# A decoder layer on one core: small loads on another queue, the residual kept in memory, the last down-projection groups by chunk, parts of x formed later

## The chip, the cores and the metric

The kernel runs on 1 core of one Trainium2 chip. The metric is the device time of one execution in microseconds. The engines are named as in the profile: PE is TensorE (its matmuls; PEld are its weight loads), DVE is VectorE, ACT is ScalarE, POOL is GpSimd, and SP is SyncE, which here does nothing but issue DMAs. ACTq and SPq are the DMA issues of ACT and SP.

## The reference

One layer of a hybrid decoder, for 1024 prompt rows and 8 sample rows (1032 rows in all, model width 1024, feed-forward width 2816), all in float32. The input is normalised first; three token mixers read it through one projection; two residual steps with a norm follow.

```python
xp = layer_norm(x_prompt, ln_in_g, ln_in_b)
xs = layer_norm(x_sample, ln_in_g, ln_in_b)
# in the layer, for each of the two:
proj = x @ w_in + b_in                       # q, k, v, o, gates i and f, u, xq, branch gates
y_m = (norm of sigmoid(o) * mLSTM(q, k, v, i, f)) @ w_m_out
y_p = pool_mix(u)                            # trailing means over 2, 4, 8, 16 rows, @ w_pool
y_x = softmax(xq mk^T) mv @ w_x_out          # mk, mv = mem @ w_mem_kv, or the cache
mix = (g0 * y_m + g1 * y_p + g2 * y_x) @ w_o
x = layer_norm(ALPHA * x + mix, ln1_g, ln1_b)
hup = x @ w_up                               # 2 * 2816 columns
c = causal depthwise convolution of width 3 over hup, + conv_b
a, b = split(c)
f = (gelu(a) * b) @ w_down
x = layer_norm(ALPHA * x + f, ln2_g, ln2_b)
```

The outputs are x for both groups and the new states (mLSTM, pooling, convolution, memory keys and values).

## The kernel before

Activations are kept feature-major: 128 features in the partitions, the 1032 rows in the free dimension, eight such tiles for a width of 1024. Float32 precision comes from splitting each operand in a high and a low part of the matmul's type and adding three products: hi·hi, hi·lo, lo·hi. xhi and xlo are the parts of the current x, whi and wlo (also whl, which holds both halves) those of a weight. The high part is a copy on ACT, the low part a subtraction on DVE (early in the program on POOL too). Rows are handled in three chunks of 384, 384 and 264 (CHUNKS), or, where a layer norm follows, in three passes of 392, 384 and 256 from the last rows to the first (PASSES).

The program is a list of units that PE works off in order (run_units, matmul L258): a unit is one tile of weights times all its chunks. Ahead of time each unit has its weights loaded and split. Between units, generators put in the other work: each step of a generator issues some instructions and yields the microseconds for which it wants to wait, counted against the matmuls issued since. So the yields and the order in which generators were added set the order of instructions on ACT, DVE, POOL and SP; each of these engines works its list off in that order. A DMA issue waits until the DMA issued eight before it in the program has landed, as well as for its data and for its buffer.

The stages, in us from the start of the span: memory keys and values (w_mem_kv) with the input norm beneath them (0 to 80); the w_in projection and the mixers (to 1236); pooling (to 1301); the w_o projection with LN1 beneath it (to 1416); the first three feed-forward tiles as plain units (to 1499); the other nineteen as Strassen products on halves (to 1897); the down-projection with LN2 beneath it (to the end).

What the change touches:

- The small parameter rows, rowsA (L319), eight loads issued by ACT at the start. The rows of x are loaded by SP between the weights of w_mem_kv (raw, L179; x, L311). memT0h, memT0l (L456, L457) are the split transposes of the memory input on ACT and DVE.
- to_features (L381 to L398) transposes normalised rows on PE (L387), applies gain and bias on ACT into tmp (L389) and splits into xhi and xlo. With spill it also writes tmp to memory. It is used for the input norm (no spill) and for LN1 (spill into x1D, eight arrays of 128 x 1032).
- wo_unit (L1378): the evacuation of w_o forms z = ALPHA·(xhi + xlo) + p in two operations on DVE (L1384, L1385). g_rows1 transposes z back to rows (L1398), takes statistics, and normalises on ACT into xn (L1410); few_to_features (L1415 to L1427) does the eight sample rows by themselves: eight small activations xs (L1422) and eight writes into x1D (L1425), all on ACT.
- g_parts (L1660 to L1710): the Strassen products need differences of quarters of x. For four values of k it loads quarters from x1D (wf, L1676), forms three differences on DVE (L1693, L1694, L1700, L1703) and splits them into tx on ACT and DVE (L1684, L1685). last_part (L1715, L1716) splits a fourth one into xhi and xlo once the plain units are done. The evacuation of a plain unit's product is hup (L1527); conv and gelu work on it as cv (L1488 to L1501).
- run_pairs (L1835 on): seven products for each half (L1776), in the order 1, 2, 6, 7, 5, 3, 4, evacuated into t, u, v and hup (L1782 to L1792). The convolution of the pair before goes on beneath them, one step (post) at four of the seven products; its result is written to gD.
- run_down (L1945): w_down in six groups of 4, 4, 4, 4, 2 and 4 tiles of k; a product (L1960) is added into z (z2 in the code, L1970). Groups 0 to 4 run over CHUNKS; group 5 runs pass by pass, so that LN2 of a finished pass (ln2_half, ln2_dev, ln2_out, L1990 to L2045) lies beneath the next. g_stages loads gD and splits it into xhi and xlo (stage, L1885, L1886).

## Time and profile before

| | |
|---|---|
| median of 3 runs | 2180.38 us (2178.87 to 2181.81) |
| the profiled execution | 2181.64 us |
| its span, first to last instruction | 2179.9 us |
| mean granted clock of PE | 0.990 |
| busy: PE, DVE, ACT, POOL | 2123.8, 1296.2, 847.2, 207.7 us |

The page's part of busy time gives each engine's time, its share of the span and its instructions. The list of waits has for each kind of wait what waited, for what, and then us in total, times, and the longest. A row of the timeline is start, length, engine, line and operation, out<-in, shapes and count, and in brackets the idle time before it with what ended it. The table of windows has for each stretch its length, the busy time and the count of PE, PEld, DVE, ACT and POOL, the clock granted to PE (1.00 is full speed), DMA's busy share and GB/s.

### The profile page before, as it was taken

To read this page: it belongs to the slowest core of one execution; us is meant where nothing else is said; L and a number is where in the kernel's file an instruction comes from. 1 tells how busy PE (TensorE), PEld (TensorE's weight loads), DVE (VectorE), ACT (ScalarE), POOL (GpSimd) and SP (SyncE) were. 2 spreads that over 40 slices of the span, in tenths; PEclk is the share of its full clock that TensorE was granted. 3 is DMA by queue.
4 is the path that set the end of the run, shared out by engine and by line. 5 is a ranking of instruction groups with operands and counts; after the bars stand their busy time and mean duration, and the time that the engine had idled before them with its cause. 6 is when DMAs were issued, how large, how long until landed. Compare 5 with 4: busy or idle time off the path is not lost.

```text
span 2179.9 us, 37597 instructions
## 1 busy us (share of the span) xinstructions
PE 2123.8 (97%) x14801; PEld 2081.2 (95%) x14801; DVE 1296.2 (59%) x2922; ACT 847.2 (39%) x1693; POOL 207.7 (10%) x329
## 2 busy tenths in 40 slices
PE   7999999999999999999999999998999999999996
PEld 6999999999999999999999999998999999999996
DVE  5734838383756655425334645748777777755457
ACT  5624343434446533332213333435555555522111
POOL 5301010101000000000003720000000000000004
PEclk9999999999999999999999999999999999999998
DMA  8231232323268575648752322444222222462302
GB/s 244 79 108 54 54 69 62 65 54 79 81 157 278 174 221 173 215 153 313 248 172 85 95 82 78 141 122 136 66 83 79 77 81 79 152 208 69 107 1 78
DMA packets 303837, 265.54 MB, mean 122 GB/s; under 512 B 19405, under 2 KB 275753, under 8 KB 303645
## 3 DMA queue, kind: packets, MB, share of 16 engines
q1 hardware_dynamic: 286763, 244.06, 37.4%
q10 hardware_dynamic: 16898, 19.09, 2.5%
q8 instruction: 116, 1.90, 0.4%
q14 instruction: 60, 0.49, 0.1%
HBM read 197.21 MB, written 66.49 MB: 121 GB/s over the span
## 4 chain that ended last, share of the span: by engine, by line
PE 85%; DVE 6%; DMA 2%; POOL 2%; ACT 2%; issue 2%; SPq 1%; ACTq 0%; POOLq 0%; DVEq 0%
PE pd L258 48%; PE pd L1776 17%; PE pd L1960 10%; PE ps L678 1%; PE ps L679 1%; PE ps L680 1%; DVE wlo L189 1%; DMA ck<-in_cache_mem_k_dram 1%; PE ps L702 1%; DMA Cs<-in_state_C_dram 1%; POOL ps L1286 1%; DMA wf<-x1D 1%; PE ps L387 0%; ACT whi L188 0%; PE ps L883 0%
## 5 line engine op out<-in xcount | busy, mean ns | idle before, releaser
L258 PE MATMUL pd<-xhi,whi 128*128 128x384 f32 (+1 forms) x1872 | 606.8, 324 | 3.3 <-ACT hup L1527 3.3
L258 PE MATMUL pd<-xlo,whi 128*128 128x384 f32 (+1 forms) x1872 | 603.9, 323 | 0.0
L258 PE MATMUL pd<-xhi,wlo 128*128 128x384 f32 (+1 forms) x1872 | 600.9, 321 | 0.0
L258 PEld LDWEIGHTS pd<-xhi,whi 128*128 128x128 f32 x1872 | 353.1, 189 | 12.8 <-issue 8.3
L258 PEld LDWEIGHTS pd<-xlo,whi 128*128 128x128 f32 x1872 | 353.2, 189 | 1.8 <-issue 1.7
L258 PEld LDWEIGHTS pd<-xhi,wlo 128*128 128x128 f32 x1872 | 353.0, 189 | 1.8 <-issue 1.7
L189 DVE TENSOR_TENSOR wlo<-raw,whi 128x512 fp32r<-128x512 f32 (+1 forms) x236 | 166.4, 737 | 275.6 <-ACT whi L188 264.4
L1960 PE MATMUL pd<-xhi,whl 128*128 128x384 f32 (+3 forms) x1056 | 249.1, 322 | 5.0 <-DVE z L1970 5.0
L1776 PE MATMUL pd<-xhi,whl 128*128 128x258 f32 x1216 | 228.0, 285 | 0.5 <-ACT v L1782 0.5
L188 ACT ACTIVATE whi<-raw 128x512 fp32r<-128x512 f32 (+1 forms) x264 | 151.4, 615 | 108.5 <-PE pd L258 80.7
L1776 PEld LDWEIGHTS pd<-xhi,whl 128*128 128x128 f32 x1216 | 192.8, 191 | 0.7 <-ACT v L1782 0.7
L1960 PEld LDWEIGHTS pd<-xhi,whl 128*128 128x128 f32 x1056 | 184.1, 189 | 6.3 <-DVE z L1970 6.2
L1617 ACT ACTIVATE whl<-wf 128x512 fp32r<-128x512 f32 (+1 forms) x181 | 107.7, 617 | 188.3 <-PE pd L1960 145.8
L1776 PE MATMUL pd<-tx,whl 128*128 128x258 f32 x1368 | 172.9, 285 | 3.4 <-DVE hup L1792 2.3
L1776 PE MATMUL pd<-xlo,whl 128*128 128x258 f32 x608 | 173.4, 285 | 2.8 <-DVE xlo L1716 2.7
L1776 PEld LDWEIGHTS pd<-tx,whl 128*128 128x128 f32 x1368 | 168.1, 190 | 4.0 <-DVE hup L1792 2.5
L1960 PE MATMUL pd<-xlo,whl 128*128 128x384 f32 (+3 forms) x528 | 169.7, 321 | 0.2 <-DVE xlo L1886 0.2
L371 POOL TENSOR_TENSOR rs<-rs,half 128x1 f32<-128x1 f32 (+2 forms) x60 | 36.7, 611 | 1218.4 <-DVE rs L370 1187.1
L1618 DVE TENSOR_TENSOR whl<-wf,whl 128x512 fp32r<-128x512 f32 (+1 forms) x181 | 122.0, 675 | 46.5 <-ACT whl L1617 46.1
L1776 PEld LDWEIGHTS pd<-xlo,whl 128*128 128x128 f32 x608 | 116.2, 191 | 3.4 <-DVE xlo L1716 3.4
L1970 DVE TENSOR_TENSOR z<-pd,z 128x384 f32<-128x384 f32 (+3 forms) x120 | 60.9, 513 | 86.5 <-PE pd L1960 86.4
L1814 DVE SCALAR_TENSOR_TENSOR cv<-hup,colB,cv 128x1023 f32<-128x1023 f32 x76 | 97.1, 1278 | 9.7 <-ACT cv L1805 9.7
(558 smaller groups left out, 3747.4 us busy)
## 6 DMA issues: line engine op xcount, KB each, us to landing
raw<-in_w_in_dram SPq DMA_DIRECT2D x72, 512.0 KB
wf<-in_w_up_dram SPq DMA_DIRECT2D x76, 256.0 KB
gD<-cv SPq DMA_DIRECT2D x22, 516.0 KB
wf<-in_w_down_dram SPq DMA_DIRECT2D x40, 256.0 KB
stage<-gD SPq DMA_DIRECT2D x18, 516.0 KB
raw<-in_w_o_dram SPq DMA_DIRECT2D x18, 512.0 KB
mx<-mixD SPq DMA_DIRECT2D x16, 516.0 KB
raw<-in_w_mem_kv_dram SPq DMA_DIRECT2D x16, 512.0 KB
```

The source lines that it names most:

```text
L188: nc.scalar.activation(s.hi[:, ks], s.raw[:, ks], AF.Copy)
L189: (nc.gpsimd if s.pool else nc.vector).tensor_sub(s.lo[:, ks], s.raw[:, ks], raw_f(s.hi[:, ks]))
L258: nc.tensor.matmul(p[:u.m, :n], lhsT=a, rhs=b, start=j == 0, stop=j == len(seq) - 1)
L371: nc.gpsimd.tensor_tensor(out=rs[:n], in0=rs[:n], in1=half[:n], op=OP.pow)
L678: nc.tensor.matmul(out, lhsT=wh, rhs=xh, start=first, stop=False)
L679: nc.tensor.matmul(out, lhsT=wh, rhs=xl, start=False, stop=False)
L1617: nc.scalar.activation(hi, src, AF.Copy)
L1618: nc.vector.tensor_sub(lo, src, raw_f(hi))
L1776: nc.tensor.matmul(p, lhsT=a[:, k], rhs=b, start=onto is None and k + n == 0, stop=k == 3 and n == 2, skip_group_check=onto is not None)
L1814: nc.vector.scalar_tensor_tensor(a, b, w, a, op0=OP.mult, op1=OP.add)
L1960: nc.tensor.matmul(p[:, :n], lhsT=a[:, k], rhs=b, start=k + i == 0, stop=k == nk - 1 and i == 2)
L1970: nc.vector.tensor_add(z, p[:, :n], z)
```

## The change

It has six parts:

1. The eight rowsA loads are issued by SP, behind the load of the first tile of x.
2. The input norm's to_features spills tmp into x0D (eight arrays of 128 x 1032), written by SP; wo_unit reads it back (xr, four buffers, two units ahead), and the evacuation of w_o is one operation on DVE.
3. few_to_features does gain and bias with two operations on DVE, and SP issues its eight writes.
4. g_parts waits 7 instead of 4 after its weights, so its steps come later.
5. In the last Strassen half, the convolution's steps come at two products instead of four.
6. Groups 4 and 5 of the down-projection both run pass by pass, first the eight units of group 4 and then those of group 5 in each pass. The weights of group 4 are kept for all three passes in tiles of the wf pool (whs). The stage loads are issued before, not after, the wait for the group two before. In LN2, the deviation (ln2_dev) of a tile comes ahead of the output of the tile before, and minus_mean (nb) moves into ln2_out.

```diff
@@ load of the parameter rows
-            nc.scalar.dma_start(rowsA[dst:dst + n], as_rows(src))
+            nc.sync.dma_start(rowsA[dst:dst + n], as_rows(src))
@@ to_features
-            tmp = cur[0].tile([128, 392], F32, tag="tmp", bufs=3, name=nm("tmp"))
+            tmp = cur[0].tile([128, 392], F32, tag="tmp", bufs=6 if b0 == LIB else 3, name=nm("tmp"))
...
-                nc.scalar.dma_start(spill[f][:, c0:c0 + n], tmp[:, :n])
+                (nc.sync if b0 == LIB else nc.scalar).dma_start(spill[f][:, c0:c0 + n], tmp[:, :n])
@@ g_ln_in
-            yield from to_features([(xt.pop(i), rows_of(i)) for i in tiles], c0, n, LIG, LIB, 1.0)
+            yield from to_features([(xt.pop(i), rows_of(i)) for i in tiles], c0, n, LIG, LIB, 1.0,
+                                   spill=x0D)
@@ wo_unit
+        def ahead():
+            c0, n = chunk
+            t = X0[c0, f] = cur[0].tile([128, 392], F32, tag="xr", bufs=4, name=nm("xr"))
+            nc.sync.dma_start(t[:, :n], x0D[f][:, c0:c0 + n])
...
-            nc.vector.scalar_tensor_tensor(z, raw_f(xhi[:, f, c0:c0 + n]), ALPHA, p[:, :n], op0=OP.mult, op1=OP.add)
-            nc.vector.scalar_tensor_tensor(z, raw_f(xlo[:, f, c0:c0 + n]), ALPHA, z, op0=OP.mult, op1=OP.add)
+            nc.vector.scalar_tensor_tensor(z, X0.pop((c0, f))[:, :n], ALPHA, p[:, :n], op0=OP.mult, op1=OP.add)
@@ few_to_features
+        nc.vector.tensor_mul(tmp, p[:, :8 * NS].rearrange("p (f b) -> p f b", f=8), by_tile(L1G))
+        nc.vector.tensor_add(tmp, tmp, by_tile(L1B))
         for f in range(8):
-            nc.scalar.activation(tmp[:, f], p[:, f * NS:(f + 1) * NS], AF.Identity,
-                                 bias=colA[:, L1B + f:L1B + f + 1], scale=colA[:, L1G + f:L1G + f + 1])
-        for f in range(8):
-            nc.scalar.dma_start(x1D[f][:, T:], tmp[:, f])
+            nc.sync.dma_start(x1D[f][:, T:], tmp[:, f])
@@ g_parts
         load_weights()
-        yield 4.0
+        yield 7.0
@@ run_pairs
-                if x in (2, 3, 5, 6):
+                if x in ((2, 3, 5, 6) if i < len(halves_) - 1 else (2, 6)):
                     post[:] = [g for g in post if next(g, g) is not g]
@@ g_stages
-            while gi > 1 and gi - 2 not in down_done:
-                yield 1.0
             j0, nk = GROUPS[gi]
             stage[gi] = place["t"].tile([128, 4, TT], F32, tag="t", name=nm("stage"))
...
+            while gi > 1 and gi - 2 not in down_done:
+                yield 1.0
+            if gi == 5:
+                for (c0, n), _ in PASSES:
+                    for k in range(nk):
+                        stage_split(gi, k, c0, c0 + n)
+                        yield 1.0
+                    ready.append(f"stage{gi}_{c0}")
+                return
@@ prepare
+        if o.small:
+            slot = None
+            t = place["wf"].tile([128, HT], F32R, tag="wf", name=nm("whs"))
+            hi, lo = t[:, :n], t[:, n:2 * n]
+            made["hold"] += 1
@@ ln2_out, g_ln2
-        p, mv, rs, nb = LP.pop(t)
+        p, mv, rs = LP.pop(t)
+        nb = minus_mean(mv, rs, m)
...
                 ln2_half(tiles[i], 1)
+                ln2_dev(tiles[i])
+                yield 1.3
             if i:
                 ln2_out(tiles[i - 1], True)
-            if i < len(tiles):
-                ln2_dev(tiles[i])
-            yield 2.4
+                yield 1.3
@@ the list of down units
-    for gi in range(5):
+    for gi in range(4):
...
+    last = [[down_weights(gi, f) for f in range(8)] for gi in (4, 5)]
+    for w in last[0]:
+        w.small = True
     for i, (chunk, tiles) in enumerate(PASSES):
-        for f in range(8):
-            downs.append(Down(5, f, last[f], chunks=(chunk,), last=i == 2))
+        for gi in (4, 5):
+            for f in range(8):
+                downs.append(Down(gi, f, last[gi - 4][f], chunks=(chunk,), last=i == 2))
```

The order of instructions at three places follows, in rows of line, operation, out<-in and size. First ACT at the start of the program before: the eight rowsA loads stand ahead of the copies of the memory input.

```order
L157 ACTIVATE warm<-ident 128x1
L319 DMA rowsA<-in_b_in_dram 32x128
L319 DMA rowsA<-in_b_in_dram 40x128
L319 DMA rowsA<-in_mh_g_dram 8x128
L319 DMA rowsA<-in_pool_scale_dram 8x128
L319 DMA rowsA<-in_ln_in_g_dram 8x128
L319 DMA rowsA<-in_ln_in_b_dram 8x128
L319 DMA rowsA<-in_ln_g_dram 8x128
L319 DMA rowsA<-in_ln_b_dram 8x128
L456 ACTIVATE memT0h_156<-ps_279 128x256
```

And SP at the start of the program after the change (raw is a w_mem_kv load, x a tile of the input).

```order
L179 DMA raw_275<-in_w_mem_kv_dram 128x8x128
L311 DMA x_208_277<-in_x_prompt_dram 128x1024
L319 DMA rowsA<-in_b_in_dram 32x128
L319 DMA rowsA<-in_b_in_dram 40x128
L319 DMA rowsA<-in_mh_g_dram 8x128
L319 DMA rowsA<-in_pool_scale_dram 8x128
L319 DMA rowsA<-in_ln_in_g_dram 8x128
L319 DMA rowsA<-in_ln_in_b_dram 8x128
L319 DMA rowsA<-in_ln_g_dram 8x128
L319 DMA rowsA<-in_ln_b_dram 8x128
L179 DMA raw_333<-in_w_mem_kv_dram 128x8x128
L311 DMA x_224_366<-in_x_prompt_dram 128x1024
```

The eight loads have moved from ACT, where nothing else was being issued, to SP, between the first and the second tile of x.

Second, DVE where the Strassen products begin: the last round of parts (k = 3) and the first xlo of last_part. Before:

```order
L1693 TENSOR_TENSOR wf_16606<-wf_16606,wf_16561 128x516
L1694 TENSOR_TENSOR wf_16561<-wf_16559,wf_16561 128x516
L1618 TENSOR_TENSOR whl_16663<-wf_16392,whl_16663 128x512
L1685 TENSOR_TENSOR tx_16270<-wf_16606,tx_16270 128x516
L1700 SCALAR_TENSOR_TENSOR wf_16559<-wf_16606,wf_16559 128x516
L1608 TENSOR_TENSOR wf_16327<-wf_16327,wf_16408 128x512
L1618 TENSOR_TENSOR whl_16679<-wf_16327,whl_16679 128x512
L1685 TENSOR_TENSOR tx_16269<-wf_16559,tx_16269 128x516
L1703 SCALAR_TENSOR_TENSOR wf_16604<-wf_16559,wf_16604 128x516
L1618 TENSOR_TENSOR whl_16699<-wf_16325,whl_16699 128x512
L1494 SCALAR_TENSOR_TENSOR cv_16656<-hup_16532,colB,cv_16656 128x1023
```

After (L1721, L1722, L1728 and L1731 are the differences, L1713 is tx, L1643 is whl, L1513 a convolution step, L1744 is xlo):

```order
L1721 TENSOR_TENSOR wf_16687<-wf_16687,wf_16646 128x516
L1722 TENSOR_TENSOR wf_16646<-wf_16644,wf_16646 128x516
L1643 TENSOR_TENSOR whl_16743<-wf_16375,whl_16743 128x512
L1513 SCALAR_TENSOR_TENSOR cv_16706<-hup_16573,colB,cv_16706 128x1023
L1713 TENSOR_TENSOR tx_16320<-wf_16687,tx_16320 128x516
L1728 SCALAR_TENSOR_TENSOR wf_16644<-wf_16687,wf_16644 128x516
L1713 TENSOR_TENSOR tx_16319<-wf_16644,tx_16319 128x516
L1731 SCALAR_TENSOR_TENSOR wf_16685<-wf_16644,wf_16685 128x516
L1513 SCALAR_TENSOR_TENSOR cv_16706<-hup_16573,colB,cv_16706 128x1022
L1513 SCALAR_TENSOR_TENSOR cv_16706<-stT,colB,cv_16706 128x8 x2
L1713 TENSOR_TENSOR tx_16321<-wf_16685,tx_16321 128x516
L1744 TENSOR_TENSOR xlo<-wf_16324,xhi 128x516
```

Two weight halves and a weight sum that stood between the steps of this round now stand ahead of it, and the convolution step that stood behind the second difference now stands ahead of the first tx.

Third, DVE at the end of the Strassen products: cv is the convolution of the pair before, xlo here the split of the first stage for the down-projection, and the hup from v the evacuation that frees the products' bank. Before:

```order
L1814 SCALAR_TENSOR_TENSOR cv_21473<-hup_21069,colB,cv_21473 128x1022
L1814 SCALAR_TENSOR_TENSOR cv_21473<-stT,colB,cv_21473 128x8
L1903 TENSOR_TENSOR xlo<-wf_21379,xhi 128x516
L1828 TENSOR_TENSOR cv_21473<-cv_21395,cv_21473 128x1032
L1903 TENSOR_TENSOR xlo<-wf_21433,xhi 128x516
L1792 SCALAR_TENSOR_TENSOR hup_21317<-pd_21520,v_21549 128x258
L1903 TENSOR_TENSOR xlo<-wf_21435,xhi 128x516
```

After:

```order
L1931 TENSOR_TENSOR xlo<-wf_21429,xhi 128x516
L1842 SCALAR_TENSOR_TENSOR cv_21523<-hup_21119,colB,cv_21523 128x1023
L1842 SCALAR_TENSOR_TENSOR cv_21523<-stT,colB,cv_21523 128x8
L1931 TENSOR_TENSOR xlo<-wf_21483,xhi 128x516
L1820 SCALAR_TENSOR_TENSOR hup_21367<-pd_21567,v_21594 128x258
L1842 SCALAR_TENSOR_TENSOR cv_21523<-hup_21119,colB,cv_21523 128x1022
L1842 SCALAR_TENSOR_TENSOR cv_21523<-stT,colB,cv_21523 128x8
L1931 TENSOR_TENSOR xlo<-wf_21485,xhi 128x516
```

The product of the two convolution halves (L1828) has moved behind this hup, out of these rows.

More of the change, by code (lines that the diff above doesn't have):

```diff
@@ L415, in g_rows_in @@
             yield 2.8
+    x0D = [DR(f"x0D{f}", [128, TT]) for f in range(8)]
     def g_ln_in():
@@ L1383, in evac @@
             z = Z[c0, f] = ZT[c0, f // per][:, f % per * n:(f % per + 1) * n]
-            nc.vector.scalar_tensor_tensor(z, raw_f(xhi[:, f, c0:c0 + n]), ALPHA, p[:, :n], op0=OP.mult, op1=OP.add)
-            nc.vector.scalar_tensor_tensor(z, raw_f(xlo[:, f, c0:c0 + n]), ALPHA, z, op0=OP.mult, op1=OP.add)
-        return Unit(split, col, 8, mov_mix, evac, chunks=(chunk,))
+            nc.vector.scalar_tensor_tensor(z, X0.pop((c0, f))[:, :n], ALPHA, p[:, :n], op0=OP.mult, op1=OP.add)
+        return Unit(split, col, 8, mov_mix, evac, chunks=(chunk,), ahead=ahead)
     XN = {}
@@ L1446, in tile_hybrid_step @@
             if i == 0 and j == 0:
-                on(units[-1], "before", lambda: next_phase("phase2"))
+                first_wo = units[-1]
         on(units[-1], "after", lambda t=tiles, i=i, c0=chunk[0]: (side.add(0, f"rows1{i}", g_rows1(c0, t)),
@@ L1450, in tile_hybrid_step, with open_wo @@
     on(units[-1], "after", lambda: side.add(0, "sconv", g_state_conv()))
+    def open_wo():
+        next_phase("phase2")
+        for u in two:
+            u()
+    two = [u.ahead for u in units[units.index(first_wo):][:2]]
+    for u in units[units.index(first_wo):][:2]:
+        u.ahead = None
+    on(first_wo, "before", open_wo)
     CA, TL = {}, {}
@@ L1561, in __init__ @@
             self.src, self.w, self.f, self.steps = src, {}, {}, steps
-            self.sums = 0
+            self.sums, self.small = 0, False
     def wf_tile(n=512):
@@ L1598, in prepare @@
     def prepare():
-        if made["obj"] == len(wq) or not slots:
+        if made["obj"] == len(wq) or not (slots or wq[made["obj"]].small):
             return False
@@ L1611, in prepare @@
             return False
-        slot = slots.pop(0)
-        t = (wp if slot == "w" else place["ex"]).tile([128, 1024], F32R, tag="w", name=nm("whl"))
         src = o.f[key]
         n = src.shape[1]
-        hi, lo = t[:, :n], t[:, 512:512 + n]
+        if o.small:
[3 more added lines that the diff above has]
+            made["hold"] += 1
+        else:
+            slot = slots.pop(0)
+            t = (wp if slot == "w" else place["ex"]).tile([128, 1024], F32R, tag="w", name=nm("whl"))
+            hi, lo = t[:, :n], t[:, 512:512 + n]
         nc.scalar.activation(hi, src, AF.Copy)
@@ L1635, in release @@
     def release(o, key):
-        slots.append(o.w[key][2])
+        if o.small:
+            made["hold"] -= 1
+        else:
+            slots.append(o.w[key][2])
     def x_part(m, k, s):
@@ L1953, in run_down @@
             if u.f == 0 and (u.gi or c0):
-                wait_for(f"stage{u.gi}")
+                wait_for(f"stage{u.gi}" if u.gi < 5 else f"stage5_{c0}")
             p = pp.tile([128, 512], F32, tag="d", bufs=3, name=nm("pd"))
@@ L2011, in ln2_dev @@
         mv, rs = mean_dev(st, 2, m)
-        LP[t] = p, mv, rs, minus_mean(mv, rs, m)
+        LP[t] = p, mv, rs
     def ln2_out(t, slow):
         m = rows_of(t)
-        p, mv, rs, nb = LP.pop(t)
+        p, mv, rs = LP.pop(t)
+        nb = minus_mean(mv, rs, m)
         y = R("y")
@@ L2034, in g_ln2 @@
                 ln2_half(tiles[i], 1)
+                ln2_dev(tiles[i])
+                yield 1.3
             if i:
                 ln2_out(tiles[i - 1], True)
-            if i < len(tiles):
-                ln2_dev(tiles[i])
-            yield 2.4
-    last = [down_weights(5, f) for f in range(8)]
+                yield 1.3
+    last = [[down_weights(gi, f) for f in range(8)] for gi in (4, 5)]
+    for w in last[0]:
+        w.small = True
     for i, (chunk, tiles) in enumerate(PASSES):
-        for f in range(8):
-            downs.append(Down(5, f, last[f], chunks=(chunk,), last=i == 2))
+        for gi in (4, 5):
+            for f in range(8):
+                downs.append(Down(gi, f, last[gi - 4][f], chunks=(chunk,), last=i == 2))
         if i == 0:
```

2 lines of the change are left out of this document (added).

## The prediction

> **What bounds the kernel now.** I read first the busy times, then the list of what TensorE waits for, then the granted clock of the stretches behind the long waits.
>
> ```profile
> PE 2123.8 (97%) x14801; PEld 2081.2 (95%) x14801; DVE 1296.2 (59%) x2922; ACT 847.2 (39%) x1693; POOL 207.7 (10%) x329
> ```
>
> TensorE is busy 97% of 2179.9 us and the change leaves its matmuls as they are. So what can be won is idle time of PE, time at half clock, and the tail. The waits, as us in total, times, longest:
>
> ```profile
> PE ps L454 <- DVE memT0l L457: 8.2, 1, 8.2
> PE ps L387 <- ACT xn L1410: 5.8, 2, 3.2
> PE pd L1960 <- DVE z L1970: 5.0, 3, 2.9
> PE pd L258 <- ACT hup L1527: 3.3, 1, 3.3
> PE pd L1776 <- DVE xlo L1716: 2.7, 2, 1.5
> PE ps L2005 <- DVE z L1970: 2.4, 2, 1.9
> PE pd L1776 <- DVE hup L1792: 2.3, 1, 2.3
> ...
> PE ps L1398 <- DVE z L1385: 1.0, 2, 0.6
> ```
>
> Every edit aims at one of these rows. Behind each long wait there are stretches of 3.4 us, or two of them, at half clock (columns: length, busy time and count of PE, PEld, DVE, ACT and POOL, clock, DMA share, GB/s):
>
> ```profile
> 1359.50:1366.30 6.80, 5.95 (x20) 5.85 (x21) 3.59 (x8) 4.87 (x8) 0.00 (x0) 0.50 0.45 121
> 1475.50:1478.90 3.40, 3.40 (x13) 3.40 (x12) 3.37 (x6) 0.84 (x2) 0.00 (x0) 0.50 0.65 205
> 1509.70:1516.50 6.80, 6.04 (x28) 6.04 (x29) 5.79 (x10) 1.81 (x4) 0.00 (x0) 0.50 0.45 132
> 1895.40:1898.80 3.40, 3.18 (x14) 3.18 (x15) 1.57 (x4) 3.21 (x6) 0.00 (x0) 0.50 0.96 303
> 2141.20:2144.50 3.30, 2.87 (x9) 2.88 (x10) 3.12 (x5) 0.78 (x1) 2.37 (x2) 0.50 0.30 117
> ```
>
> A matmul takes twice its time there, so such a stretch costs half of PE's busy time in it: 3.0, 1.7, 3.0, 1.6 and 1.4 us.
>
> **A. Small loads to SP.**
>
> ```profile
> 14.34 0.28 ACTq L319 DMA_DIRECT2D rowsA<-in_ln_b_dram  x1
> 14.67 1.21 ACT L456 ACTIVATE memT0h<-ps 128x256 fp32r<-128x256 f32 x4 [12.37 <-DMA rowsA<-in_ln_in_g_dram]
> ...
> 9.40 0.43 SPq L179 DMA_DIRECT2D raw<-in_w_mem_kv_dram  x1
> ...
> 39.94 0.33 PE L387 MATMUL ps<-ident,x 128*128 128x128 f32 x1 [1.86 <-DVE x L375]
> ```
>
> ScalarE issues its last rowsA load at 14.34 and only then begins memT0h, for which PE waited 8.2 us from 7.38. Without its DMAs it can begin there: 14.67 - 7.38 = 7.3 us earlier at most. But SP now stands in those waits: in the program each issue waits on the semaphore that the DMA eight before it raises when it has landed, so the fifth w_mem_kv load, behind the eight, goes out at about 14.6 instead of 9.40. Every load behind it falls back too, by less and less as the queue fills again, and so does x, whose third tile PE waits for at 39.94. That tile cannot come the full 7.3 us earlier; between 0 and 7.3 I take 5, since the loads lose part of the delay again. PE, 7.3 us ahead, waits for it longer than now and gets a half-clock stretch (1.7 by the 3.4-us rows above); the x loads that then queue behind writes of x0, which wait for ScalarE's tmp, may cost 0 to 1.5, I take 0.8. 5 - 1.7 - 0.8 = **2.5**, bounds 0 and 7.3.
>
> **B. Residual from memory, and C. few_to_features off ScalarE.**
>
> ```profile
> 1355.37 0.60 ACT L1422 ACTIVATE xs<-ps,colA 128x8 f32<-128x8 f32 x2
> ...
> 1357.09 2.38 ACTq L1425 DMA_DIRECT2D x1D<-xs  x5
> 1359.52 1.44 ACT L1410 ACTIVATE xn<-ps,nb,rs 128x512 f32<-128x512 f32 x2 [2.05 <-DVE z L1385]
> ...
> 1360.35 0.48 PE L387 MATMUL ps<-ident,xn 128*128 128x128 f32 x1 [3.17 <-ACT xn L1410]
> ...
> 1320.00:1340.00 20.00, 20.00 (x117) 19.71 (x116) 9.53 (x18) 2.25 (x4) 0.00 (x0) 1.00 0.25 72
> ```
>
> From 1355.37 to 1359.47 ScalarE does eight small activations and eight issues while xn stands behind them; PE idles 3.17 us and then runs 6.8 us at half clock (3.0). With two DVE operations and SP's issues instead, xn can start some 2.7 us earlier (its row names 2.05 us of idle time that falls away as well), which about closes the gap: 6.2. The z wait of 1.0 goes with the second STT. On the other side: eight writes of 0.48 us each (2.38 / 5) now stand on SP before the next w_o load, 3.8 us; PE is not waiting for w_o loads here, so between 0 and 3.8, near 0: I take 0.5. The first w_o loads also stand behind two reads of x0D. The other xn gap of the 5.8 (2.6 us) stays, and the free phase of the clock's stretches can give it a drop it did not have (1.7, about two in three: 1.1). The 4.2 MB written and 4.2 MB read (8 x 128 x 1032 x 4 bytes) lie in stretches like the last row, where DMA is 25% busy: nothing. Against the 7.2: 0.5 + 1.1 and 0.6 for the loop's rest. **5.0**, bounds 2 and 7.2.
>
> **D. Parts of x later.**
>
> ```profile
> 1461.15 2.89 SPq L1573 DMA_DIRECT2D wf<-in_w_up_dram  x4
> ...
> 1467.55 0.70 DVE L1693 TENSOR_TENSOR wf<-wf,wf 128x516 f32<-128x516 f32 x1 [8.65 <-DMA wf<-x1D]
> ...
> 1473.73 0.47 ACT L1527 ACTIVATE hup<-pd 128x384 f32<-128x384 f32 x1
> ...
> 1502.70 0.38 ACT L1782 ACTIVATE t<-pd 128x258 f32<-128x258 f32 x1
> ...
> 1505.77 0.69 DVE L1716 TENSOR_TENSOR xlo<-wf,xhi 128x516 fp32r<-128x516 f32 x1
> ...
> 1467.50:1505.70 38.20, 33.75 (x220) 33.19 (x220) 34.98 (x54) 22.29 (x43) 0.00 (x0) 0.96 0.49 146
> ```
>
> The evacuation hup at 1473.73 stands behind two tx copies that wait for DVE; PE's 3.34 us gap and the 1.7 of clock come from that. Now the copies stand behind hup, so hup comes about 1.5 to 2.7 us earlier. But this does not set the end of the stage. DVE does: it is busy 34.98 of the 38.20 us from 1467.55 to the first xlo, for which PE waits again (1.5 and 1.2 us), and ScalarE's t, behind the last tx, makes the first tx matmul wait. The same work must be done before those, and DVE now starts on weight halves, whose four loads stand on SP behind the x1D loads (1461.15): some 2 us after 1467.55 (an estimate: 4 x 256 KB at the 303 GB/s of the 1895.40 row take 3.5 us, part of which is over by then). Two wlo that stood behind its first step, 0.6 us each by their 512 columns (xlo above, 516, takes 0.69), go ahead of it. The last round of tx (last k) ends up in one row behind everything, each step going DVE to ScalarE to DVE; the x1D loads for it are issued only after the round before. I count 2 us of late start, 1.2 saved, and 0 to 4 us more idle time in these handoffs, of which I take 2.2: xlo 3 us later on the same scale. PE, earlier by the gap that closed, idles it all away before the first tx matmul; that long idle time has its half clock inside the wait, which gives back half of the 3.0. **-1.5**; at best +5 (3.34 and 1.7 all kept), at worst -5.
>
> **E. Last Strassen half.**
>
> ```profile
> 1893.40 1.22 DVE L1828 TENSOR_TENSOR cv<-cv,cv 128x1032 f32<-128x1032 f32 x1
> ...
> 1895.15 0.41 DVE L1792 SCALAR_TENSOR_TENSOR hup<-pd,v 128x258 f32<-128x258 f32 x1
> ...
> 1895.62 0.58 PE L1776 MATMUL pd<-tx,whl 128*128 128x258 f32 x1 [2.32 <-DVE hup L1792]
> ```
>
> PE's matmuls feeding that hup end at 1893.3. In the new order the multiply cv (1893.40) no longer stands ahead of it; a convolution step and two xlo still do. hup comes some 1.1 us earlier, the gap falls to 1.2. With half of the idle time gone the half clock (1.6) should not follow: **2.6**, bounds 0 and 3.9. The clock stood at 0.50 right behind a gap of 2.32 us. The Trainium skill ("TensorE: Matmul & The Clock Gate", "Why this matters for your kernels") asks for no idle gaps above about 3 us; by it the 2.32 us would have cost no clock, and E would be 1.1 and the time 2169.8. The trace disagrees in this place. That page's Part 1 calls the window free-running, 3413 ns long, and with that the 3.4 us stretches agree.
>
> **F. Last two groups by chunk.**
>
> ```profile
> 2135.09 0.55 POOL L371 TENSOR_TENSOR rs<-rs,half 128x1 f32<-128x1 f32 x1 [0.94 <-DVE rs L370]
> ...
> 2140.36 0.55 POOL L371 TENSOR_TENSOR rs<-rs,half 128x1 f32<-128x1 f32 x1 [0.94 <-DVE rs L370]
> ...
> 2135.75 0.55 DVE L1970 TENSOR_TENSOR z<-pd,z 128x384 f32<-128x384 f32 x1
> ...
> 2166.38 1.10 PE L2005 MATMUL ps<-ident,z 128*128 128x128 f32 x6 [0.50 <-DVE z L1970]
> ```
>
> A tile of LN2 takes 5.27 us (2135.09 to 2140.36); four take 21.1, the middle pass has 8 x 12 matmuls at about 0.175 us (the last row of B has 117 in 20.00 us), 16.8. So z, behind nb and y on DVE, comes late, up to the 2.91 us in the waits. With group 4 in the pass there are 8 x 6 matmuls more (8.4 us) and eight z of 0.55 (4.4): 25.5 of DVE under 25.2 of matmuls, and the transposes beside them. The waits (5.0 + 2.4) should halve, not vanish, since tiles still come early in a pass; a drop of the clock is as likely as now. The tail behind 2167.48, 12.4 us, has the same operations. **3.5**, bounds 0 and 9 (7.4 and 1.4).
>
> **Sum.** 2.5 + 5.0 - 1.5 + 2.6 + 3.5 = 12.1. Against the profiled execution, 2181.64: 2169.5; the runs' median, 2180.38, lies 1.26 below that execution, so **2168.3**.
>
> **Rivals.**
> - *DVE keeps pace in D.* The handoffs fit into its 3.2 us of idle time and the closed gap is kept: +5 for -1.5, 2161.8. Against it: 35 of 38 us busy.
> - *Front and end give it back.* SP's late loads eat all of A, the z waits move instead of halving: 2174.3. For it: the queue of A, and DVE as full under the passes as before.
> - *It does not do what it says:* D at -5, A and F nothing, B and C 2.5, E 1.1: -1.4 and 2181.8.
> - *Slower: weights run dry in the first pass.* Sixteen weights must be there within 25.8 us of matmuls (8 x 18 at 0.179, the 0.175 by 392/384). If they come one by one, at up to 2.7 us each (four w_up loads issued at 1461.15, the last in use at 1471.97 at the latest), 43 us are needed and PE loses 17: 2185.6. It decides once more than 16 us come through. Against it: the whole of group 3 ahead, 8 units of 12 matmuls on each chunk, some 45 us, in which they can be loaded.
>
> **Numbers.** Forecast 0.52, DVE keeps pace 0.13, given back 0.17, nothing 0.12, slower 0.06. A measurement here tells apart about 0.2%, 4.4 us: faster 0.82 (the first three), same 0.12, slower 0.06. The range runs from below the second case into the fourth, 2158 to 2180, and leaves out the slower case, much of the fourth and the outer bounds of D and F.
>
> **What would show it.** Right: the L454 wait is gone and an x wait on L387 near 30 us has grown; no 3.17 us gap beside xs; the hup wait, some 8 us earlier than now, below 2 us, but PE waiting 5 us or more for t just before the first tx matmul; the hup L1792 wait near 1.2 us with full clock behind it; z waits of 3 to 4 us in all. Wrong: a t wait under 2 us (D gains), a wait for whl or whs at L1960 (the slower case), or raw loads named in waits between 1300 and 1416 (B and C smaller).

## The result, and the profile after

| | before | after |
|---|---|---|
| median of 4 runs | 2180.72 us (2178.87 to 2181.81) | 2162.50 us (2161.90 to 2166.63) |
| ratio after / before | | 0.992, 95% interval 0.9905 to 0.9936 |
| profiled execution | 2181.64 us | 2166.63 us |
| its span | 2179.9 us | 2164.5 us |

The change is 18.2 us faster in the medians; 12.1 had been forecast (2168.3 us), and the time lies in the range. The profiled execution is the longest of the four after the change, so the traces show only 15.4 us of span; where the rest lies is told with the first experiment.

The page's busy times after the change, then the list of what PE waits for (us in total, times, longest):

```profile
PE 2120.8 (98%) x14801; PEld 2080.7 (96%) x14801; DVE 1282.9 (59%) x2908; ACT 847.3 (39%) x1693; POOL 211.3 (10%) x329
```

```profile
PE pd L1804 <- ACT t L1810: 8.2, 1, 8.2
PE ps L387 <- DVE x L375: 6.4, 3, 4.5
PE pd L1995 <- DVE z L2005: 3.0, 2, 2.1
PE ps L387 <- ACT xn L1419: 2.4, 1, 2.4
...
PE pd L258 <- ACT hup L1546: 1.8, 1, 1.8
...
PE pd L1804 <- DVE hup L1820: 0.8, 1, 0.8
...
PE ps L2040 <- DVE z L2005: 0.2, 1, 0.2
```

The 8.2 us for memT0l is gone, and an x wait of 4.5 has come. Of two xn waits one is left. The last hup (L1820, before L1792) cost 2.3 and costs 0.8. The z waits fell from 7.4 to 3.2. Against this stands one new row at the top: PE waits 8.2 us for t, just ahead of the first tx matmul.

PE runs 14801 matmuls in every version, and up to the last two groups in the same order. So the start of the same matmul in two traces can be subtracted, and a stage's gain is how that difference grows over the stage. This table is worked out in that way from the profiled executions, in us against before (minus is gained): A from 0 to 60 us, the mixers to 1300, B and C (w_o and LN1) to 1460, D to 1516, E to 2010 (E's own place, 1885 to 1899, with nothing else happening behind it), F to the last matmul, and the tail behind it (12.4 us before). The runs below the first row are the experiments.

```
                        A mixers    B+C      D      E      F   tail   span
after                -3.8    0.1   -4.7    2.4   -3.3   -4.6   -1.5  -15.4
e0_after             -4.2    3.3   -9.1    3.1   -3.2   -6.2   -1.5  -17.8
e1_parts_early       -4.2    2.3   -9.0   -1.7   -3.2   -4.7   -1.4  -21.9
e2_rows_on_act        2.1    1.0   -7.6    3.5   -3.2   -6.2   -1.5  -11.9
e3_post_four         -3.9   -2.4   -4.8    2.7   -0.2   -4.7   -1.4  -14.7
e4_down_before       -2.6    2.0   -6.1    2.4   -3.2    1.3    0.0   -6.2
e5_few_on_act        -3.8    3.2   -1.0    3.1   -3.3   -4.7   -1.5   -8.0
e6_residual_split    -3.7   -2.3   -6.4    2.4   -3.3   -6.2   -1.2  -20.7
e7_ln2_before        -3.5   -1.6   -9.0    2.5   -3.3   -2.1    0.0  -17.0
e8_chunk_before      -2.8    2.2   -9.2    2.6   -3.3   -7.7   -1.5  -19.7
e9_rows_later        -3.4    2.0   -8.9    0.1   -3.3   -6.2   -1.4  -21.1
e10_t_first          -3.8    3.1   -6.4    2.7   -3.2   -4.7   -1.5  -13.8
e11_all              -4.8    1.0   -5.7   -1.0   -3.2   -4.7   -1.4  -19.8
```

The mixers' column, where the change does nothing, shows how far one profiled execution can be trusted: it runs from -2.4 to 3.3.

### The profile page after: what moved, and what is told of

The parts are those of the page before. It is cut to its first block, busy times and chain, and to the rows that moved or that the text cites. A ratio compares the mean times of both kernels' runs of the same rounds, so it can differ in the third digit from the quotient of the medians.

```text
span 2164.5 us, 37648 instructions
## 1 busy us (share of the span) xinstructions
PE 2120.8 (98%) x14801; PEld 2080.7 (96%) x14801; DVE 1282.9 (59%) x2908; ACT 847.3 (39%) x1693; POOL 211.3 (10%) x329
## 4 chain that ended last, share of the span: by engine, by line
PE 85%; DVE 5%; DMA 4%; ACT 2%; SPq 1%; issue 1%; POOL 1%; ACTq 0%; DVEq 0%; POOLq 0%
PE pd L258 48%; PE pd L1804 18%; PE pd L1995 11%; PE ps L681 2%; PE ps L682 1%; PE ps L683 1%; DMA g2r<-gD 1%; SPq L179 1%; PE ps L705 1%; DMA x<-in_x_prompt_dram 1%; DMA Cs<-in_state_C_dram 1%; POOL ps L1289 1%; PE ps L387 1%; DVE cv L1513 1%; DVE wlo L189 1%
## 5 line engine op out<-in xcount | busy, mean ns | idle before, releaser
L1995 PE MATMUL pd<-xhi,whl 128*128 128x384 f32 (+3 forms) x960 | 225.5, 321 | 3.0 <-DVE z L2005 3.0
L1804 PEld LDWEIGHTS pd<-xhi,whl 128*128 128x128 f32 x1216 | 190.6, 189 | 1.0 <-ACT v L1810 0.7
L1995 PEld LDWEIGHTS pd<-xhi,whl 128*128 128x128 f32 x960 | 167.5, 189 | 3.6 <-DVE z L2005 3.5
L1642 ACT ACTIVATE whl<-wf 128x512 fp32r<-128x512 f32 x173 | 104.4, 626 | 158.6 <-PE pd L1995 117.8
L1995 PE MATMUL pd<-xlo,whl 128*128 128x384 f32 (+3 forms) x480 | 154.3, 321 | 0.0
L1643 DVE TENSOR_TENSOR whl<-wf,whl 128x512 fp32r<-128x512 f32 x173 | 118.8, 687 | 47.9 <-ACT whl L1642 47.5
```

Source lines behind the costliest of these rows:

```text
L1642: nc.scalar.activation(hi, src, AF.Copy)
L1643: nc.vector.tensor_sub(lo, src, raw_f(hi))
L1804: nc.tensor.matmul(p, lhsT=a[:, k], rhs=b, start=onto is None and k + n == 0, stop=k == 3 and n == 2, skip_group_check=onto is not None)
L1995: nc.tensor.matmul(p[:, :n], lhsT=a[:, k], rhs=b, start=k + i == 0, stop=k == nk - 1 and i == 2)
```

## The experiments

Each kernel is the changed one with one part undone or moved. Kernels that did not run side by side are compared through their ratio to runs of before on the same chip.

**The changed kernel again**, with no edit.

> The changed kernel once more, as the measure for the runs beside it. Both theories: 2162 to 2164 us, 0.992 of the kernel before. If the 2166.6 of the profiled execution was only the phase of the clock's windows, single times near 2166 turn up here too.

Measured: 2164.66 us against 2182.74, ratio 0.9926 (0.991 to 0.9943). Single executions ran from 2162.37 to 2172.70 us, so times near 2166 do turn up. Its trace is 2.4 us shorter than the first one, with B and C at 9.1 instead of 4.7 and F at 6.2 instead of 4.6 (and 3.2 lost in the mixers). The windows of the two tell why (columns as before: the clock is the third number from the end). First execution, then this one (a drop is a stretch in which this clock is lower):

```profile
1392.50:1395.90 3.40, 3.40 (x20) 3.40 (x19) 2.99 (x6) 1.94 (x4) 0.00 (x0) 0.58 0.22 81
1426.50:1433.30 6.80, 6.80 (x37) 6.39 (x36) 3.19 (x11) 1.68 (x3) 0.00 (x0) 0.55 0.24 80
2144.40:2147.80 3.40, 3.40 (x20) 3.40 (x20) 0.77 (x2) 0.00 (x0) 0.23 (x1) 0.56 0.20 77
```

```profile
1392.50:1395.90 3.40, 1.51 (x13) 1.51 (x14) 1.65 (x5) 2.15 (x4) 0.00 (x0) 1.00 0.64 193
1426.50:1433.30 6.80, 6.80 (x57) 6.25 (x56) 3.77 (x13) 2.26 (x4) 0.00 (x0) 1.00 0.34 114
2144.40:2147.80 3.40, 3.40 (x31) 3.40 (x31) 2.01 (x4) 0.00 (x0) 0.00 (x0) 1.00 0.20 77
```

The same program got about half clock in these places in one execution and full clock in the other. The first two windows cost 0.42 x 3.4 + 0.45 x 6.8 = 4.5 us and the third 0.44 x 3.4 = 1.5: the differences of B and C (4.4) and of F (1.6). So a stage's gain has to be read with the drops that fell into it.

**D undone: parts of x early.**

```diff
-        yield 7.0
+        yield 4.0
```

> The changed kernel with the parts of x formed as early as before (wait 4 instead of 7). Theory 'DVE sets the start of the Strassen products': faster than the changed kernel by 2 to 4.5 us (2158 to 2160.5), the wait for t falls from 8.2 to 1 to 2 us, the hup wait grows from 1.8 to 3.3 us. Rival 'the closed hup gap is kept': slower by 3 to 5 us (2165.5 to 2167.5).

Measured: 2161.00 us, ratio 0.9903 (0.9888 to 0.9918), 3.7 below the changed kernel in the same comparison; the intervals still touch. D goes from +2.4 or +3.1 to -1.7. The waits there, after the edit:

```profile
PE pd L258 <- ACT hup L1546: 3.6, 1, 3.6
...
PE pd L1804 <- DVE xlo L1744: 2.7, 2, 1.5
...
PE pd L1804 <- ACT t L1810: 1.3, 1, 1.3
```

The early hup wait is back at 3.6 (3.3 before the change), but only 1.3 of the 8.2 us for t stays. So part 4 trades 1.8 us of one wait (3.6 to 1.8) for 6.9 of another, less 2.7 for xlo. That is a loss of 2.4 in waits alone. The clock adds to it. The two windows behind the long wait in the changed kernel, and the one behind the 1.3 us after the edit:

```profile
1499.50:1503.00 3.50, 2.31 (x10) 2.31 (x11) 3.46 (x7) 3.27 (x7) 0.00 (x0) 0.50 0.14 41
1503.00:1506.30 3.30, 3.30 (x19) 3.30 (x19) 3.30 (x7) 2.87 (x5) 0.00 (x0) 0.60 0.34 95
```

```profile
1492.00:1495.50 3.50, 2.85 (x23) 2.86 (x24) 3.46 (x6) 3.50 (x10) 0.00 (x0) 1.00 0.88 291
```

With PE busy for 2.31 us at 0.50 and 3.30 at 0.60, 0.50 x 2.31 + 0.40 x 3.30 = 2.5 us go; with the early parts none. 2.4 + 2.5 = 4.9, beside 4.1 to 4.8 by the table. The two later runs with early parts (e9_rows_later, e11_all) have D at 0.1 and -1.0: each had a drop of 3.4 us behind its xlo waits. So part 4 loses 2.3 to 5.2 us between any two of these traces.

**The last third part behind t**, with the late start kept.

```diff
             split(6, k, x11)
...
-            split(4, k, x21)
+            if k < 3:
+                split(4, k, x21)
+            else:
+                later.append(lambda: split(4, 3, x21))
...
     def last_part():
         k = last_part.k
+        if k == 1:
+            later.pop()()
```

> The changed kernel with its late start of the parts of x, but the last round's third part is rounded after ScalarE has copied t, not before. Theory (t waits its turn on ScalarE behind the last handed-off part, and that part alone comes about 2 us behind the one that TensorE needs): the wait for t falls from 8.2 to about 6.5 us, the kernel is 1.5 to 2 us faster than the changed one. Rival (t only stands where the sixth product's own part would hold TensorE anyway): the wait keeps its length under another name, the time within 0.5 us of the changed kernel.

Measured: 2167.58 us, ratio 0.9926 (0.9906 to 0.9946), the same as the changed kernel. Its list of waits has:

```profile
PE pd L1810 <- ACT t L1816: 6.5, 1, 6.5
...
PE pd L1810 <- DVE xlo L1750: 0.9, 1, 0.9
```

The first half of the theory held: the wait fell by 1.7 us. The second did not: D is +2.7, as in the other runs with the late start (2.4 to 3.5). PE starts earlier and is stopped again at xlo, which stands behind the same work: its waits for t, xlo and hup in the stage are 9.8 us in all, where the changed kernel has 10.0. ScalarE's rows in the changed kernel show what the stage waits for:

```profile
1493.99 0.63 ACT L1712 ACTIVATE tx<-wf 128x516 fp32r<-128x516 f32 x1 [1.32 <-DVE wf L1721]
1497.73 0.63 ACT L1712 ACTIVATE tx<-wf 128x516 fp32r<-128x516 f32 x1 [3.10 <-DVE wf L1728]
...
1499.73 0.63 ACT L1712 ACTIVATE tx<-wf 128x516 fp32r<-128x516 f32 x1 [1.09 <-DVE wf L1731]
1500.27 0.37 ACT L1810 ACTIVATE t<-pd 128x258 f32<-128x258 f32 x1
```

Three tx copies of the last round, each behind a difference from DVE, together with ScalarE's waits for them, fill the time from 1492.67 to 1500.27, with ScalarE idle for 5.5 us of it. DVE's rows, first where it comes to the weights, then the first difference and the first xlo, and the window between these two:

```profile
1461.26 0.69 DVE L1607 TENSOR_TENSOR wf<-wf,wf 128x512 f32<-128x512 f32 x1 [4.20 <-DMA wf<-in_w_up_dram]
...
1462.47 0.69 DVE L1721 TENSOR_TENSOR wf<-wf,wf 128x516 f32<-128x516 f32 x1
...
1501.81 0.69 DVE L1744 TENSOR_TENSOR xlo<-wf,xhi 128x516 fp32r<-128x516 f32 x1
```

```profile
1462.40:1501.80 39.40, 29.26 (x179) 28.56 (x178) 33.18 (x51) 20.06 (x39) 0.00 (x0) 0.88 0.40 122
```

DVE is busy 33.18 of 39.40 us, so 6.2 idle, where between the same two operations it was busy 34.98 of 38.20 before, 3.2 idle. PE's matmuls come 8.4 us earlier here than before the change when this stage begins, so the first difference, at 1467.55 before, is 3.3 us late against them, and the first xlo, at 1505.77 before, 4.4 us late. Neither engine is full: the handoffs from one to the other are in a row and begin too late.

**A undone: rows on ScalarE.**

```diff
-            nc.sync.dma_start(rowsA[dst:dst + n], as_rows(src))
+            nc.scalar.dma_start(rowsA[dst:dst + n], as_rows(src))
```

> The changed kernel with the eight rowsA loads issued by ACT again. Theory 'A is worth the difference between memT0h starting early and x coming late': slower by 2.5 to 4 us (2165 to 2166.5), L457 waits again 8 us, the x wait near 30 us falls from 4.5 to about 2. Rival 'the queue of SP gives all of it back': within 1 us of the changed kernel.

Measured: 2170.07 us, ratio 0.9947 (0.9935 to 0.9959), 5.4 above the changed kernel and more than the 2.5 to 4 expected. The memT0l wait is back with 8.0 us, and the x waits are 4.2 in all (longest 1.9). A is +2.1 instead of about -3.8. So the move of the rows alone is worth 5.4 (the medians) to 5.9 us. Against before, the front even loses 2.1 here; the new writes of x0D are the only other change in it, though with the rows on SP nothing is gained by leaving them out (B undone, below).

**Rows still on SP, but behind the third x tile** (with the parts of x early).

```diff
                 load_x(0)
-                load_rows()
                 mem_transposes()
...
                 load_x(2)
+                load_rows()
```

> The row loads on SyncE are issued behind the third x tile instead of the first (and the parts of x are formed as early as before the change). Theory (SyncE stands in the row loads while x tiles 1 and 2 wait, and that is why the x wait near 30 us stays at 4.5 to 6.2 us): that wait falls to under 3 us and the kernel gains 1.5 to 3 us on the variant with the parts formed early alone (2161.0): 2158 to 2159.5. Rival (x comes late because the memory system is full, not because of who is in front): the wait stays at 4.5 to 6 us, the time at 2160 to 2162.

Measured: 2161.58 us, ratio 0.9901 (0.9884 to 0.9917), as the variant with early parts alone. The theory fell: the x wait is 5.1 us, within the 4.5 to 6.9 of the runs that leave this part as it is. The timeline tells where it comes from. SP and DVE in the changed kernel:

```profile
14.66 1.05 SPq L311 DMA_DIRECT2D x<-in_x_prompt_dram  x2
15.75 9.32 SPq L179 DMA_DIRECT2D raw<-in_w_mem_kv_dram  x5
25.19 1.66 SPq L311 DMA_DIRECT2D x<-in_x_prompt_dram  x1
```

```profile
25.05 1.79 DVE L375 TENSOR_SCALAR x<-x,mv,rs 128x1024 f32<-128x1024 f32 x1 [0.17 <-POOL rs L371]
31.77 1.29 DVE L363 BATCH_NORM_STATS2 st<-x 128x6 f32<-128x512 f32 x2 [4.93 <-DMA x<-in_x_prompt_dram]
...
33.41 0.80 DVE L375 TENSOR_SCALAR x<-x,mv,rs 128x1024 f32<-128x1024 f32 x1
```

And with the rows behind the third tile:

```profile
9.81 1.89 SPq L311 DMA_DIRECT2D x<-in_x_prompt_dram  x2
...
18.59 6.40 SPq L179 DMA_DIRECT2D raw<-in_w_mem_kv_dram  x5
25.11 1.53 SPq L311 DMA_DIRECT2D x<-in_x_prompt_dram  x1
```

```profile
31.11 1.29 DVE L363 BATCH_NORM_STATS2 st<-x 128x6 f32<-128x512 f32 x2 [5.49 <-DMA x<-in_x_prompt_dram]
...
32.75 0.80 DVE L375 TENSOR_SCALAR x<-x,mv,rs 128x1024 f32<-128x1024 f32 x1
```

The loads of the second and third tile went out 4.9 us earlier and nothing came of it. In g_rows_in the statistics of a tile (L363) stand ahead of the normalisation of the one before (L375). So DVE waits for the fourth tile before it normalises the third, for which PE waits. The fourth is issued at 25.1 us in both, behind five raw loads in which SP stands (9.32 us, or 6.40 when it comes to them later). That the fourth tile sets the wait is read from these rows; a kernel with the two operations in the other order was not run.

**C undone: the eight sample rows on ScalarE.**

```diff
-        nc.vector.tensor_mul(tmp, ...)
-        nc.vector.tensor_add(tmp, tmp, by_tile(L1B))
         for f in range(8):
-            nc.sync.dma_start(x1D[f][:, T:], tmp[:, f])
+            nc.scalar.activation(tmp[:, f], p[:, f * NS:(f + 1) * NS], AF.Identity, ...)
+        for f in range(8):
+            nc.scalar.dma_start(x1D[f][:, T:], tmp[:, f])
```

> The changed kernel with few_to_features' eight activations and eight writes on ACT again. Theory 'they stood ahead of xn': slower by 4 to 6.5 us (2168.5 to 2171 where the changed kernel has 2164.7), a wait of about 3 us for xn at L1419 comes back beside them, with half clock behind it. Rival 'that gap was the loop of ACT and DVE in LN1, not the small work': slower by at most 2 us.

Measured: 2170.63 us, ratio 0.996 (0.9945 to 0.9975), by the ratios 7.4 us above the changed kernel, somewhat more than expected. The gap of before is back, in the same place:

```profile
1356.90 2.32 ACTq L1434 DMA_DIRECT2D x1D<-xs  x5
1359.27 1.44 ACT L1419 ACTIVATE xn<-ps,nb,rs 128x512 f32<-128x512 f32 x2 [2.05 <-DMA x1D<-xs]
```

```profile
1360.10 0.33 PE L387 MATMUL ps<-ident,xn 128*128 128x128 f32 x1 [3.15 <-ACT xn L1419]
```

B and C together gain 1.0 in this trace, where the others have 4.7 to 9.2. By the traces C is worth 3.7 to 8.2 us, by how many drops of the clock fall into the stage.

**B undone: the residual from xhi and xlo.**

```diff
-            nc.vector.scalar_tensor_tensor(z, X0.pop((c0, f))[:, :n], ALPHA, p[:, :n], ...)
+            nc.vector.scalar_tensor_tensor(z, raw_f(xhi[:, f, c0:c0 + n]), ALPHA, p[:, :n], ...)
+            nc.vector.scalar_tensor_tensor(z, raw_f(xlo[:, f, c0:c0 + n]), ALPHA, z, ...)
...
-                                   spill=x0D)
```

> The changed kernel without x0D: the residual from xhi and xlo in two operations again, nothing written or read. Theory 'the second STT costs its one wait of 0.6 us': slower by 0.3 to 1.5 us, the x wait near 30 us unchanged. Rival 'the 8.4 MB and the place of the writes on SP cost something': faster by 1 to 3 us, with smaller x waits between 30 and 65 us.

Measured: 2163.54 us, ratio 0.9924 (0.9909 to 0.9939), the same as the changed kernel. A z wait of 0.9 us in all is back in LN1; in the front the two small x waits (0.6 and 1.3) are gone. The long one is 6.0, within the 4.5 to 6.9 of the runs that keep x0D. B moves some two microseconds about and is worth nothing that can be measured.

**E undone: the convolution at four products in the last half** (profiled, without an interval).

```diff
-                if x in ((2, 3, 5, 6) if i < len(halves_) - 1 else (2, 6)):
+                if x in (2, 3, 5, 6):
```

> The changed kernel with the convolution's steps at four products in the last Strassen half again. Theory: the wait for hup at L1820 goes from 0.8 back to 2.3 us and 3.4 us of half clock stand behind it; the stretch is 3 us longer. Rival 'the clock's drop was chance': 2.3 us of wait and full clock behind it, 1.5 us longer.

Measured: 2167.0 us, span 2165.1. E falls from 3.3 to 0.2, by 3.1. The wait for hup is 2.3 us as before, and the two windows behind it are, in the changed kernel and then here:

```profile
1885.80:1889.20 3.40, 2.56 (x21) 2.36 (x21) 2.94 (x7) 3.08 (x7) 0.00 (x0) 1.00 1.05 321
1889.20:1892.60 3.40, 3.40 (x22) 3.40 (x22) 3.40 (x7) 3.40 (x7) 0.00 (x0) 1.00 1.21 300
```

```profile
1885.80:1889.20 3.40, 2.37 (x14) 2.37 (x15) 2.57 (x7) 3.40 (x7) 0.00 (x0) 0.84 0.78 240
1889.20:1892.60 3.40, 3.40 (x15) 3.40 (x15) 2.83 (x6) 1.62 (x5) 0.00 (x0) 0.66 1.07 317
```

1.5 us of the gain is the wait (2.3 to 0.8); the other 1.7 = 0.16 x 3.4 + 0.34 x 3.4 is the clock, which does not drop behind the shorter gap. Both traces with the old order had this drop; the last section shows why a gap of 2.3 us can also go without one.

**F undone, whole and in halves.** Part 6 of the change has two edits: which units run in which pass, and the order inside LN2. First both undone:

```diff
-    for gi in range(4):
+    for gi in range(5):
...
-        for gi in (4, 5):
-            for f in range(8):
-                downs.append(Down(gi, f, last[gi - 4][f], chunks=(chunk,), last=i == 2))
+        for f in range(8):
+            downs.append(Down(5, f, last[f], chunks=(chunk,), last=i == 2))
...
-                ln2_dev(tiles[i])
-                yield 1.3
             if i:
                 ln2_out(tiles[i - 1], True)
-                yield 1.3
+            if i < len(tiles):
+                ln2_dev(tiles[i])
+            yield 2.4
```

> The changed kernel with the down-projection and LN2 of before (group 4 over all chunks, old order in LN2). Theory 'the longer passes cover LN2': slower by 4 to 7 us (2166.5 to 2169.5), z waits 7 us again, half clock near the middle pass. Rival 'it was only the phase of the clock': slower by at most 2 us and z waits as in the changed kernel, 3 us.

Measured: 2175.44 us, ratio 0.9968 (0.9957 to 0.9979), 10.8 above the changed kernel: more than expected. F with its tail goes from -6.1 or -7.7 (the two traces of the changed kernel) to +1.3.

Then only the order inside LN2 undone (the last lines of the diff above, and minus_mean back in ln2_dev):

> The changed kernel with the old order inside LN2 (deviation after the output of the tile before, nb with the deviation), groups 4 and 5 by chunk as in the change. Theory 'the longer passes do it': slower by 0 to 2.5 us, z waits 3 to 5 us. Rival 'the order in LN2 does it': slower by 4 to 8 us, z waits 7 us as before.

Measured: 2167.56 us, ratio 0.9946 (0.9929 to 0.9962), by the ratios 4.4 us above the changed kernel. The rival held: F and tail are -2.1, the tail is 12.4 us as before the change, and z waits of 7.3 us (5 times) are back beside one of 0.2.

Last, only the passes undone (the diff's other lines), LN2 in its new order:

> The last two groups of the down-projection in the order of before, the order inside the last LayerNorm kept as changed. The run without both parts lost 7.5 us of the profile between the last rows and the end, the one without the LayerNorm's order 4.1. If the two add up, this one loses 3 to 4 us on the changed kernel: a z wait of 2 to 3 us back between the passes, and the tail behind the last matmul near 11 us as in the changed kernel. Rival (the chunk order is worth all of it, and the LayerNorm's order only matters inside it): it loses 6 to 8 us.

Measured: 2162.47 us, ratio 0.9914 (0.9898 to 0.9931). Neither expectation held. Without the chunk order nothing is lost: F and tail are -9.2, better than with it, and the z waits between the passes are 1.2 us in all. So by the table the order inside LN2 gains 9.2 + 1.3 = 10.5 us where the passes are those of before, and the chunk order, on top of it, gives back 1.5 to 3.1. With the old LN2 the same chunk order seems to gain 2.1 + 1.3 = 3.4, but that is all clock: the run with both parts undone had two drops of 3.4 us in F, 1.7 lost in each, and the one with the old LN2 alone had none. In what PE waits for z the chunk order gains nothing with the old LN2 (7.2 us without it, 7.5 with it) and loses 2.0 with the new one (1.2 and 3.2). The LN2 order takes 6.0 or 4.3 us off these waits, and 1.5 off the tail. The medians alone do not tell the changed kernel from this one; the traces do, by these rows, first of the changed kernel, then of this one, where PE waits longest for z:

```profile
2142.51 0.39 PE L1995 MATMUL pd<-xhi,whl 128*128 128x256 f32 x1 [2.14 <-DVE z L2005]
```

```profile
2146.26 0.39 PE L1988 MATMUL pd<-xhi,whl 128*128 128x256 f32 x1 [0.88 <-DVE z L1998]
```

Why is the order inside LN2 worth so much? DVE and POOL rows of one tile before the change:

```profile
2130.39 0.16 DVE L379 SCALAR_TENSOR_TENSOR nb<-mv,rs 128x1 f32<-128x1 f32 x1 [0.66 <-POOL rs L371]
...
2132.91 1.79 DVE L2023 SCALAR_TENSOR_TENSOR y<-y,rs,gb 128x512 f32<-128x512 f32 x1
```

```profile
2131.50 1.28 POOL L2026 TENSOR_TENSOR y<-y,gb 128x512 f32<-128x512 f32 x1 [1.14 <-ACT y L2021]
2132.86 1.29 POOL L2027 TENSOR_TENSOR y<-y,gb 128x512 f32<-128x512 f32 x1
```

And of one tile after it:

```profile
2133.76 0.75 DVE L2059 SCALAR_TENSOR_TENSOR y<-y,rs,gb 128x512 f32<-128x512 f32 x1
```

```profile
2134.00 1.66 POOL L2062 TENSOR_TENSOR y<-y,gb 128x512 f32<-128x512 f32 x1 [1.04 <-ACT y L2057]
```

Before, DVE stood still 0.66 us or more in each tile for rs, and then its second y operation, 0.75 us long by itself, took 1.79: POOL's operation on the same tile had begun 0.05 us earlier, and DVE ended 0.55 us behind it (2134.70 and 2134.15). After, rs comes while DVE does other work, DVE's operation begins first, and it is POOL's that grows, from 1.28 to 1.66. In the tile shown that is 0.66 + 1.04 = 1.7 us of DVE between PE and its next z. Not every tile gains as much: over all nine, DVE's waits for rs, what the second y operation takes beyond 0.75 us and what nb takes beyond its 0.15 come to 13.1 us before and 4.6 after. How much of LN2's gain is the wait for rs and how much the longer operations was not measured apart. The Trainium skill ("SBUF — State Buffer", "SBUF: two separate sides") says that VectorE and GpSimd share a pair of ports under an exclusive lock, for which one of two operations waits out the other. These rows agree, though POOL's times are rough in these profiles and the 0.05 us alone prove little. They agree even for the smallest operation: a 128x1 nb that takes 0.15 us elsewhere takes 1.26 at 2138.97 in the changed kernel, under a POOL operation that runs from 2138.55 to 2140.22.

**Early parts, rows behind the third tile, last third part behind t, all together.**

> Both together on the changed kernel: rows behind the third x tile, parts formed early, the last third part behind t. If both theories hold, 2157 to 2159 (1 us below the rows alone, since the wait for t is only 1.3 us where the parts are early); if neither does, 2160.5 to 2162, the variant with early parts alone.

Measured: 2162.27 us, ratio 0.9901 (0.9881 to 0.9921). The t wait is 1.1 us, the xlo waits 3.6: neither addition gives anything on top of the early parts. So the three kernels with early parts (0.9901 to 0.9903) cannot be told apart; the simplest of them is the change without its part 4. The change without its parts 4 and the chunk order was not run.

## Why the prediction was right

It named where the time would go, and its list of signs holds: the L454 wait gone with a grown x wait (4.5), no gap beside xs, hup at 1.8, a long t wait (8.2 for "5 us or more"), 0.8 with full clock behind it at the last hup, z waits of 3.2 for "3 to 4". The rival that DVE keeps pace in D fell, and so did the rival that the weights run dry: no wait for whl or whs is in the list. What was wrong are sizes, and in two steps, the third x tile in A and all of F, the reason.

- **A, 2.5 forecast; 2.6 to 4.8 measured.** The direction and the new x wait were right. The step "so does x, whose third tile PE waits for" was not: the third tile's normalisation stands behind the statistics of the fourth, and moving loads 4.9 us ahead changed nothing.
- **B and C, 5.0 forecast; 4.7 in the profile of after, up to 9.2 in others.** C is all of it (3.7 to 8.2 by its removal), B nothing; the forecast had put 1.0 on B's z wait, which B does remove but gives back in the front. The drop of the clock in the other xn gap, taken at 1.1, came in the first trace and stayed away in the second.
- **D, -1.5 forecast; -2.4 to -3.5 measured.** The right sign and the right mechanism: the closed hup gap is idled away before the first tx matmul. The term "0 to 4 us more idle time in these handoffs, of which I take 2.2" measured 3.0 (6.2 of DVE's idle time, 3.2 before). Mis-sized most was "2 us of late start": the first difference is 3.3 us late, behind DVE's wait of 4.20 us for w_up. With 1.8 saved (34.98 to 33.18) that makes the first xlo 4.4 us late instead of 3. "DVE does", because it is busy 34.98 of 38.20, fits the stage less after the change: what sets its end is when the row of handoffs begins and how long it is.
- **E, 2.6 forecast; 3.1 by its removal.** Half of it is the clock, as reckoned; by the rule that the prediction cites from the Trainium skill ("TensorE: Matmul & The Clock Gate", "Why this matters for your kernels") only the 1.5 us of the wait would have been won. The windows of that experiment disagree with it a second time: 0.84 and 0.66 behind a gap of 2.3 us.
- **F, 3.5 forecast; 6.1 and 7.7 measured with the tail.** This is the step that failed most. It held LN2's 5.27 us a tile fixed ("four take 21.1") and the tail at "the same operations", and looked for the gain in the chunk order. The runs showed the reverse: the order inside LN2 shortens a tile and takes 1.5 us off the tail, and the chunk order gives some of it back. That the z waits came to 3.2 us, as forecast, is luck: with the chunk order alone they are 7.5. The rows from which this could have been read, DVE's 0.66 us of idle time for rs and 1.79 us for an operation of 512 columns, are in the trace of before.

The sum, 12.1, stands against 15.4 us of span in the first trace: F lacked 2.6 and A 1.3, E 0.7, and D's loss was taken 0.9 too small. The 17.8 of the second trace has 4.4 more in B and C by the clock alone.

## What to carry to other kernels

When a step on a critical chain is priced by its duration in the trace, ask first whether that duration is its own: an operation that takes twice its usual time beside another engine is a wait in disguise, and reordering may remove it. Delaying work to unblock one evacuation moves the wait to the next consumer of that work, so look for who needs the last piece of it, and count its handoffs in a row. And undo a change's parts one by one: here one part lost 3.7 us in the medians, one was worth nothing, and one, the chunk order, gave time back once another was there.
